# Four pairs of tiles by seven products instead of six in the last projection, with an ordered queue on each vector engine

## The chip, the cores and the metric

The kernel runs on one core of a Trainium2 chip. The metric is the time of one execution on the device, in microseconds, lower being better. The core has a matrix engine (TensorE, PE in the profile, with its weight loads as PEld), three engines that work element by element (VectorE as DVE, ScalarE as ACT, GpSimd as POOL), a queue that issues transfers (SyncE, SP) and 16 DMA engines between the off-chip memory and the core's own memory. Each engine works through its own instructions in program order and waits on semaphores that the others raise.

## The reference

The reference is one block of a sequence model on 512 tokens of width 1024: a norm, one wide projection, three token mixers, a gated merge, an output projection, and then a feed-forward part with a short convolution. All is float32. The change touches the last step only, the product by `w_down`, and what brings its operands:

```python
def conv_glu_ffn(h, w_up, w_conv, b_conv, w_down):
    a, u = jnp.split(h @ w_up, 2, axis=-1)
    return (jax.nn.gelu(dwconv3(a, w_conv, b_conv)) * u) @ w_down
...
    x = x + conv_glu_ffn(rms_norm(x, ffn_norm_g[l]), w_ffn_up[l], w_ffn_conv[l], b_ffn_conv[l], w_ffn_down[l])
return rms_norm(x, final_norm_g)
```

The hidden width is 2816, so `w_down` has 22 tiles of 128 rows and 1024 columns.

## The kernel before

**Precision.** Every float32 operand is split in a high part (a rounded copy, made by ScalarE) and a low part (the operand less the high part, made by VectorE). `mm3` (L309 to L312) makes of one product three matmuls: high by high, high by low, low by high.

**Stages.** Up to 735 us the program runs the mixers and, from L1251, a loop over 22 hidden tiles (the up stage): two projections of 24 matmuls each for a tile, then the convolution and the activation on VectorE and ScalarE, one multiply of each tile on GpSimd (L1274). From 735 us it multiplies by `w_down` (the down stage, L1354 to L1406), and after the last matmul a short tail finishes the last norm and stores.

**The down stage.** The columns are two halves of 512, the tokens two halves of 256. Of the 22 hidden tiles the first `2*NSP` are taken in pairs (p = 0 to NSP-1): a pair, the two token halves and the two column halves form a two-by-two block product, which is done with seven products in place of eight (`FORMS`, L48, numbered 1 to 7). Each of the seven forms needs a sum or a difference of token blocks (`emit_form`: a difference on VectorE, then a split in two tiles `uf`) and, except forms 2 and 5, a sum or a difference of two weight blocks. The other NOK hidden tiles are ordinary: for each column half, four token tiles by one weight tile. An item of the work is either `("s", form, pair)`, 6 matmuls of 512 columns, or `("k", column half, tile)`, 12 of them. The last three ordinary tiles of the second column half (`HELD`) are kept back and run token tile by token tile at the end. `down_items` (L54) writes the order of the items by hand: part 0 has forms 2, 4, 5, 7 and the ordinary tiles of the left half, part 1 has forms 1, 3, 6 and those of the right half; the numbers behind each form say after which pairs an ordinary tile follows.

**Weights of an item.** `weights(key)` is called as the item begins and emits, for later items: the load (`emit_raw`, on SP's queue, 256 KB for one block), the second block of a weight sum (`emit_sum`: a DMA on GpSimd's queue that adds into the tile already loaded, L236), the token block of a form (`emit_form`), and the split of the weight tile two items ahead (`emit_split`, L270 on ScalarE and L271 on VectorE). For form 1 the two weight blocks are loaded side by side and VectorE subtracts them (L247). Split weights lie in a ring of four tiles `w`; loads lie in large units (`up`, 14 units of 2112 columns for the whole kernel), four blocks in each. The first NSP items and the rest of the program use a smaller ring of three (`wr`).

**Results.** Forms 1 to 5 gather in two banks each (`at`), and `add` (L1303) adds a bank into the output blocks `C_`, four adds for a form, written behind the form's last matmul. Forms 6 and 7 and the ordinary tiles gather in four other banks (`mm`). `left` (L1320) takes the square sum of a finished left half and multiplies it by the gain, on GpSimd (L1323).

**What sets the order.** Instructions of one engine stand in an order that a scheduler chooses from the program's order and its own estimate of when operands are there; it may put a later-written instruction ahead. Only where `tc.issue_after` is used does one stand behind another by rule: before, that is so for the adding DMAs on GpSimd, behind each other and behind the multiply L1274 of the last hidden tile. The units of loads are given out in the scheduler's order too, as soon as one is free.

Of the kernel before, what the change touches and what calls it, by code (L numbers as in the profile page):

```python
# [22 lines left out]
M = 256  # L23
DFF = 2816
FT = DFF // P
NSP = 6
NOK = FT - 2 * NSP
HELD = 3
HC = D // 2
# [100 lines left out]
def hybrid_block(ctx, tc, xT, memT, wflat, vecs, gbias, nabias, out):  # L130
# [51 lines left out]

    raws, split = {}, {}
    RAW_AHEAD, SPLIT_AHEAD = 3, 1
    st = {"raw": 0, "sum": DOWN0, "form": DOWN0, "split": 0}
    uraw = []

    def emit_raw(i):
        key, n = BLOCKS[i]
        _, off, _ = BINDEX[key]  # L190
        src = wflat[off:off + P * n].rearrange("(p n) -> p n", p=P)
        if i < DOWN0 + NSP:
            r = wp.tile([P, BW], F32, tag="raw", name=nm("wr"), bufs=3)
        else:
            both = key[:2] == ("s", 1)
# [33 lines left out]

    ur, uf = [], {}  # L230

    def emit_sum(i):

        if i in st:
            with tc.issue_after(st["g"]):
                st["g"] = G.dma_start(raws[i], st.pop(i)[:, HC:], accum_op=ALU.add).ins  # L236

    def emit_form(i):

        key, n = BLOCKS[i]  # L240
        if key[0] != "s":
            return
        a, a2, _, w2, sign = FORMS[key[1]]
        p = key[2]
        if sign < 0:
            r = raws[i]
            V.tensor_tensor(r[:, :HC], r[:, :HC], r[:, HC:2 * HC], op=ALU.subtract)  # L247
        if p % 2 == 0:
            v = ur[p // 2][:, :4 * S].rearrange("p (q k s) -> p q k s", q=2, k=2)
            q2 = lambda t: t.rearrange("p (q s) -> p q s", q=2)  # L250
            src = v[:, :, a[1], a[0] * M:(a[0] + 1) * M]
            if a2:
                d = q2(scr())
                V.tensor_tensor(d, src, v[:, :, a2[1], a2[0] * M:(a2[0] + 1) * M], op=ALU.subtract)
                src = d
            h, l = [tp.tile([P, S], F32R, tag="E", name=nm("uf"), bufs=EB) for _ in range(2)]
            A.activation(q2(h), src, AF.Copy)
            V.tensor_tensor(q2(l), src, q2(h).bitcast(F32), op=ALU.subtract)
            uf[key[1], p // 2] = h, l

    def emit_split(i):
        key, n = BLOCKS[i]
        r = raws.pop(i)
        if i >= DOWN0:
            if key[0] == "k" and key[1] == 1 and key[2] >= NOK - HELD:
                h, l = lastw(key[2] - NOK + HELD)
            else:
                w = wp.tile([P, WT], F32R, tag="w", name=nm("w"), bufs=4)
                h, l = w[:, :HC], w[:, HC:2 * HC]
            A.activation(h, r[:, :HC], AF.Copy)  # L270
            V.tensor_tensor(l, r[:, :HC], h.bitcast(F32), op=ALU.subtract)  # L271
            split[i] = h, l
            return
        c, hs = halves(i)
# [972 lines left out]
    ou = [unit(F32R) for _ in range(NOK // 2)]  # L1247
    oq = lambda i: ou[i // 4][:, i % 4 * S:(i % 4 + 1) * S]
    UH, UL = [oq(2 * j) for j in range(NOK)], [oq(2 * j + 1) for j in range(NOK)]
    res, turns = {}, {}  # L1250
    for f in range(FT):  # L1251
        if f == 0:
# [18 lines left out]
        V.scalar_tensor_tensor(sq, sq, GC, c, op0=ALU.add, op1=ALU.mult)  # L1271
        A.activation(sq, sq, AF.Tanh, scale=GK)
        V.scalar_tensor_tensor(c, sq, 1.0, c, op0=ALU.add, op1=ALU.mult)  # L1273
        st["g"] = G.tensor_tensor(c, c, rb2, op=ALU.mult).ins  # L1274
        if f > 0:
            pu = pu1 if f == 1 else proj(("uu", f), HH, HL)
        if f < 2 * NSP:
            V.scalar_tensor_tensor(ur[f // 4][:, f % 4 * S:(f % 4 + 1) * S], pu, 0.5, c, op0=ALU.mult, op1=ALU.mult)
        else:
            V.tensor_tensor(c, pu, c, op=ALU.mult)  # L1280
            split_act(UH[f - 2 * NSP], UL[f - 2 * NSP], c, 0.5)
# [21 lines left out]
    def add(t, g, ps, op=ALU.add, cs=slice(0, HC)):  # L1303

        c = cv(t, g)[:, cs]
        if (t, g) in res:
            V.tensor_tensor(f4(c), res.pop((t, g)), f4(ps), op=op)
        else:
            V.tensor_tensor(c, c, ps, op=op)  # L1309

    def sums(src, v0):

# [7 lines left out]
    def left(t):  # L1320

        v1[t] = sums(cv(t, 0), EPS)
        G.tensor_tensor(cv(t, 0), cv(t, 0), gfin[0], op=ALU.mult)  # L1323

    def finish(t, ps):

# [2 lines left out]
        if t < NT - 1:  # L1329
# [21 lines left out]
            3: ((0, 1, ALU.add), (1, 1, ALU.add)), 4: ((1, 0, ALU.add), (0, 0, ALU.add)),  # L1351
            5: ((0, 0, ALU.add), (0, 1, ALU.subtract))}
    last = NT - 1
    for n, key in enumerate(DOWN):  # L1354
        wh, wl = weights(key)
        if key[0] == "s":
            _, i, p = key
            if p == 0 and i < 6:
# [6 lines left out]
            if i < 6 and p == NSP - 1:  # L1365
                for th, g, op in adds[i]:
                    for u in range(2):
                        add(2 * th + u, g, pm[u], op)
                if i == 1:
                    for t in range(2):  # L1370
                        left(t)
            continue
        _, g, j = key
        if j == 0:
# [2 lines left out]
        if not held:  # L1377
# [3 lines left out]
                    j == NOK - 1 if g == 0 else t == last and j == NOK - HELD - 1)  # L1381
            if g == 0 and j == NOK - 1:
                for t in range(NT):
                    add(t, 0, px[t])
                for t in range(2, NT):
                    left(t)
            continue
        res["w", j] = wh, wl
        if j < NOK - 1:
            continue  # L1390
        add(last, 1, px[last])
        for t in range(NT):
            tsl = slice(t * P, (t + 1) * P)
# [118 lines left out]
```

## Time and profile before

| | |
|---|---|
| median of 3 runs | 872.5 us (870.56 to 872.68) |
| profiled execution | 871.15 us |
| its span, first to last instruction | 869.4 us |
| before and behind the span | 1.75 us |
| TensorE busy, share of the span | 851.0 us, 98% |
| VectorE, ScalarE, GpSimd busy | 619.4, 464.1, 160.1 us |
| down stage, first to last matmul | 735.08 to 860.4 us |

The page's busy time of PE counts a matmul from its start to a modelled end, so 98% does not say that TensorE runs at its pace; the stretches in which it works at half clock count as busy too. Three views carry the reading: a table of stretches with the busy time of each engine, the instructions in order of time, and the waits of one engine for another. In a row of the table of stretches the numbers are the length, then for PE, PEld, DVE, ACT and POOL the busy time and in brackets the count of instructions, then the granted TensorE clock, the busy share of the 16 DMA engines and GB/s. In a row of the instructions in order of time they are the start, the duration, engine, line, operation, tiles (out<-in), and in square brackets the idle time ahead of it with what ended it.

### The profile page before, as it was taken

How to read it: one execution, taken by the hardware profiler on the slowest of the kernel's cores; microseconds unless marked ns; L12 is line 12 of the kernel's file. 1: busy time of each engine (PE TensorE's matmuls, PEld its weight loads, DVE VectorE, ACT ScalarE, POOL GpSimd, SP SyncE). 2: the span in 40 equal slices, each digit the busy share in tenths (PEclk: the TensorE clock that was granted, in tenths of full speed). 3: DMA queues.
4: the chain of work that ended last, by engine and by line, in shares of the span. 5: the costliest groups of instructions: out<-in, count | busy, mean ns of one | idle time of the engine just before them, and what ended most of it. 6: DMA issues, size and time to landing. Idle time of an engine off the chain costs nothing.

```text
span 869.4 us, 12253 instructions
## 1 busy us (share of the span) xinstructions
PE 851.0 (98%) x4044; PEld 713.2 (82%) x4044; DVE 619.4 (71%) x1235; ACT 464.1 (53%) x975; POOL 160.1 (18%) x243
## 2 busy tenths in 40 slices
PE   9999999999999999999999999999999999899885
PEld 7898888988888888888888888888888888787764
DVE  7699677874467668997585567766666668877663
ACT  7465556775355658887544444444444445444342
POOL 2001100000104810742001202111111111221401
PEclk9999999999999999999999999999999999999999
DMA  8237644643435846887523423544432225975932
GB/s 271 96 101 226 210 160 144 206 135 98 133 122 171 226 137 212 228 241 213 194 97 124 142 85 100 162 145 139 143 98 96 97 92 174 245 203 154 253 74 98
DMA packets 76978, 135.76 MB, mean 156 GB/s; under 512 B 10217, under 2 KB 35433, under 8 KB 76913
## 3 DMA queue, kind: packets, MB, share of 16 engines
q1 hardware_dynamic: 65808, 122.22, 43.4%
q0 software_dynamic: 10816, 12.61, 7.7%
q8 instruction: 32, 0.52, 0.3%
q14 instruction: 34, 0.27, 0.1%
q10 hardware_dynamic: 288, 0.14, 0.1%
HBM read 120.23 MB, written 14.70 MB: 155 GB/s over the span
## 4 chain that ended last, share of the span: by engine, by line
PE 89%; DMA 3%; issue 3%; DVE 3%; ACT 1%; POOL 1%; SPq 0%; POOLq 0%; DVEq 0%; ACTq 0%
PE mm L311 25%; PE mm L310 25%; PE mm L312 25%; DMA u<-wflat 3%; PE at L311 3%; PE at L312 2%; PE at L310 2%; DVE w L271 1%; PE at L958 1%; PE at L791 1%; PE at L793 1%; PE at L775 1%; POOL s L1274 0%; PE at L925 0%; PE at L924 0%
## 5 line engine op out<-in xcount | busy, mean ns | idle before, releaser
L310 PE MATMUL mm<-u,w 128*128 128x512 f32 (+1 forms) x912 | 353.8, 388 | 0.0
L312 PE MATMUL mm<-u,w 128*128 128x512 f32 (+1 forms) x912 | 352.0, 386 | 0.0
L311 PE MATMUL mm<-u,w 128*128 128x512 f32 (+1 forms) x912 | 351.9, 386 | 0.0
L285 ACT ACTIVATE w<-wr 128x512 fp32r<-128x512 f32 (+1 forms) x256 | 159.9, 628 | 145.7 <-PE mm L312 110.8
L286 DVE TENSOR_TENSOR w<-wr,w 128x512 fp32r<-128x512 f32 (+2 forms) x257 | 176.1, 689 | 69.8 <-ACT w L285 66.8
L312 PEld LDWEIGHTS mm<-u,w 128*128 128x128 f32 x912 | 171.3, 188 | 35.4 <-DVE w L286 0.7
L310 PEld LDWEIGHTS mm<-u,w 128*128 128x128 f32 x912 | 171.5, 188 | 33.7 <-ACT u L316 0.3
L311 PEld LDWEIGHTS mm<-u,w 128*128 128x128 f32 x912 | 171.4, 188 | 33.3 <-DVE u L317 0.5
L604 POOL DMA_DIRECT2D u<-nav_d x128 | 62.3, 506 | 101.0 <-PE at L958 51.9
L1274 POOL TENSOR_TENSOR s<-s,rb 128x512 f32<-128x512 f32 x22 | 37.9, 1721 | 190.0 <-DVE s L1273 182.3
L271 DVE TENSOR_TENSOR w<-u,w 128x512 fp32r<-128x512 f32 x53 | 40.5, 779 | 23.5 <-ACT w L270 23.3
L270 ACT ACTIVATE w<-u 128x512 fp32r<-128x512 f32 x53 | 32.9, 626 | 41.3 <-PE mm L312 26.6
L311 PE MATMUL mm<-w,u 128*128 128x512 f32 x116 | 46.1, 397 | 3.5 <-DVE w L271 3.5
L310 PE MATMUL mm<-w,u 128*128 128x512 f32 x116 | 46.2, 398 | 0.0
L312 PE MATMUL mm<-w,u 128*128 128x512 f32 x116 | 45.9, 396 | 0.0
L236 POOL DMA_DIRECT2D u<-wflat x24 | 21.4, 1175 | 62.4 <-DVE u L1309 27.3
L311 PEld LDWEIGHTS mm<-w,u 128*128 128x128 f32 x116 | 22.2, 192 | 8.9 <-DVE w L271 4.3
L497 ACT ACTIVATE s<-pad,vec 128x512 f32<-128x512 f32 x30 | 24.4, 813 | 5.4 <-DVE pad L495 4.4
L311 PE MATMUL at<-w,uf 128*128 128x512 f32 x60 | 24.3, 404 | 2.9 <-DVE w L271 2.9
L312 PEld LDWEIGHTS mm<-w,u 128*128 128x128 f32 x116 | 22.2, 191 | 4.7
L1242 POOL TENSOR_TENSOR acc<-acc,s 128x512 f32<-128x512 f32 x7 | 9.0, 1290 | 92.4 <-ACT s L1241 92.4
L310 PEld LDWEIGHTS mm<-w,u 128*128 128x128 f32 x116 | 22.2, 192 | 4.6
(301 smaller groups left out, 1197.3 us busy)
## 6 DMA issues: line engine op xcount, KB each, us to landing
wr<-wflat SPq DMA_DIRECT2D x124, 512.0 KB, 3.4
u<-wflat SPq DMA_DIRECT2D x50, 256.0 KB, 5.4
td<-s SPq DMA_DIRECT2D x160, 64.0 KB, 2.0
U<-td SPq DMA_DIRECT2D x40, 256.0 KB, 3.6
s<-xT SPq DMA_DIRECT2D x24, 256.0 KB, 4.4
u<-wflat POOLq DMA_DIRECT2D x24, 256.0 KB, 8.4
nab<-nabias SPq DMA_DIRECT2D x16, 256.0 KB, 3.9
u<-nav_d POOLq DMA_DIRECT2D x128, 32.0 KB, 3.6
```

The source lines that it names most:

```text
L236: st["g"] = G.dma_start(raws[i], st.pop(i)[:, HC:], accum_op=ALU.add).ins
L270: A.activation(h, r[:, :HC], AF.Copy)
L271: V.tensor_tensor(l, r[:, :HC], h.bitcast(F32), op=ALU.subtract)
L285: A.activation(h[:, u:v], src, AF.Copy)
L286: V.tensor_tensor(l[:, u:v], src, h[:, u:v].bitcast(F32), op=ALU.subtract)
L310: PE.matmul(ps, lh, rh, start=start, stop=False)
L311: PE.matmul(ps, lh, rl, start=False, stop=False)
L312: st["mm"] = PE.matmul(ps, ll, rh, start=False, stop=stop).ins
L497: A.activation(t1, pad[:, 0:512], AF.Identity, scale=vcol(w, i), bias=vcol(b, i))
L604: G.dma_start(vw[r * 32:(r + 1) * 32, i * 256:(i + 1) * 256], nav_v[hf, r, CW[b]:CW[b] + 32, hp * 256:(hp + 1) * 256])
L1242: G.tensor_tensor(acc2, acc2, sq, op=ALU.add)
L1274: st["g"] = G.tensor_tensor(c, c, rb2, op=ALU.mult).ins
```

## The change

It does five things.

- `NSP` is 4 in place of 6: eight hidden tiles are taken in pairs by seven products, and 14 in place of 10 are ordinary. The lists of `down_items` put one ordinary tile behind almost every pair of a form.
- `in_turn` issues an instruction of VectorE, ScalarE or GpSimd behind the last one that it issued on the same engine. The differences and splits of token blocks, the splits of weights, the adds and the adding DMAs go through it, so that they stand on each engine in the order in which they are written.
- `emit_form` is cut in two: `emit_diff` (differences of token blocks and of form 1's weights, up to 3 and then 4 items ahead) and `emit_form` (their splits, 3 ahead); weights are split between the two. The adding DMAs are asked for 7 items ahead in place of 5.
- The adds of a finished form or column half go on a list, `todo`; at each item one of them is emitted, or two while more than two are waiting. The multiply of `left` moves from GpSimd to VectorE.
- In the up stage the units of ordinary hidden tiles are taken one at a time; hidden tiles 8 to 11 are now split there (L317 and L316 of the kernel before) where they were stored whole (L1278).

```diff
-NSP = 6
+NSP = 4
...
-                if p in at:
+                for _ in range(at.count(p)):
...
-    part(0, ((2, (4, 5)), (4, (1, 3, 5)), (5, (2, 5)), (7, (1, 3, 5))))
-    part(1, ((1, (2, 4, 5)), (3, (2, 5)), (6, (2, 5))))
+    part(0, ((2, (3, 3)), (4, (0, 1, 2, 3)), (5, (0, 1, 2, 3)), (7, (0, 1, 2, 3))))
+    part(1, ((1, (1, 1, 2, 3)), (3, (0, 1, 2, 3)), (6, (0, 1, 3))))
...
+OWN_SUM = (1,)
...
+    chain = {}
+
+    def in_turn(eng, what, *a, **k):
+
+        with tc.issue_after(chain[eng]) if eng in chain else ExitStack():
+            chain[eng] = getattr({"V": V, "A": A, "G": G}[eng], what)(*a, **k).ins
+
     def emit_sum(i):

         if i in st:
-            with tc.issue_after(st["g"]):
-                st["g"] = G.dma_start(raws[i], st.pop(i)[:, HC:], accum_op=ALU.add).ins
+            in_turn("G", "dma_start", raws[i], st.pop(i)[:, HC:], accum_op=ALU.add)
...
-            V.tensor_tensor(r[:, :HC], r[:, :HC], r[:, HC:2 * HC], op=ALU.subtract)
+            in_turn("V", "tensor_tensor", r[:, :HC], r[:, :HC], r[:, HC:2 * HC], op=ALU.add if sign > 0 else ALU.subtract)
...
+    def emit_form(i):
+
+        key, n = BLOCKS[i]
+        if key[0] == "s" and key[2] % 2 == 0:
+            f = key[1], key[2] // 2
             h, l = [tp.tile([P, S], F32R, tag="E", name=nm("uf"), bufs=EB) for _ in range(2)]
-            A.activation(q2(h), src, AF.Copy)
-            V.tensor_tensor(q2(l), src, q2(h).bitcast(F32), op=ALU.subtract)
-            uf[key[1], p // 2] = h, l
+            in_turn("A", "activation", q2(h), uf[f], AF.Copy)
+            in_turn("V", "tensor_tensor", q2(l), uf[f], q2(h).bitcast(F32), op=ALU.subtract)
+            uf[f] = h, l
...
-            A.activation(h, r[:, :HC], AF.Copy)
-            V.tensor_tensor(l, r[:, :HC], h.bitcast(F32), op=ALU.subtract)
+            in_turn("A", "activation", h, r[:, :HC], AF.Copy)
+            in_turn("V", "tensor_tensor", l, r[:, :HC], h.bitcast(F32), op=ALU.subtract)
...
-        while st["sum"] <= min(i + 5, st["raw"] - 1):
+        while st["sum"] <= min(i + 7, st["raw"] - 1):
             emit_sum(st["sum"])
             st["sum"] += 1
+        while st["diff"] <= min(i + 3, last):
+            emit_diff(st["diff"])
+            st["diff"] += 1
+        while st["split"] <= min(i + (2 if st["split"] >= DOWN0 else SPLIT_AHEAD), last):
+            emit_split(st["split"])
+            st["split"] += 1
         while st["form"] <= min(i + 3, last):
             emit_form(st["form"])
             st["form"] += 1
-        while st["split"] <= min(i + (2 if st["split"] >= DOWN0 else SPLIT_AHEAD), last):
-            emit_split(st["split"])
-            st["split"] += 1
+        while st["diff"] <= min(i + 4, last):
+            emit_diff(st["diff"])
+            st["diff"] += 1
...
-        G.tensor_tensor(cv(t, 0), cv(t, 0), gfin[0], op=ALU.mult)
+        in_turn("V", "tensor_tensor", cv(t, 0), cv(t, 0), gfin[0], op=ALU.mult)
...
+    todo = []
+
+    def work(n):
+
+        for _ in range(min(n, len(todo))):
+            todo.pop(0)()
+
     for n, key in enumerate(DOWN):
         wh, wl = weights(key)
+        work(2 if len(todo) > 2 else 1)
...
-                        add(2 * th + u, g, pm[u], op)
+                        todo.append(lambda t=2 * th + u, g=g, ps=pm[u], op=op: add(t, g, ps, op))
```

The diff does not show where the scheduler now puts the instructions; three places of the built programs do. In their rows stand the line, the operation and the tiles, out<-in, with the number of each tile; L238 is the line of `in_turn`, so a row there is told by its tiles.

The first place is VectorE near the start of the down stage, from the low part of the weights of form 4's first pair to that of its second pair. Before, `w_7349` and `w_7364` are these two; `s_` are differences of token blocks and `u_7246` is an output block that takes adds:

```order
L271 TENSOR_TENSOR w_7349<-u_7283,w_7349 128x512
L254 TENSOR_TENSOR s_7466<-u_5381 128x512
L254 TENSOR_TENSOR s_7496<-u_5382 128x512
L254 TENSOR_TENSOR s_7541<-u_5383 128x512
L254 TENSOR_TENSOR s_7586<-u_5381 128x512
L1307 TENSOR_TENSOR u_7246<-U_6173,at_7256 128x512
L1307 TENSOR_TENSOR u_7246<-U_6260,at_7257 128x512
L1307 TENSOR_TENSOR u_7246<-U_6509,at_7256 128x512
L1307 TENSOR_TENSOR u_7246<-U_6591,at_7257 128x512
L271 TENSOR_TENSOR w_7364<-u_7283,w_7364 128x512
```

After, the same two are `w_7320` and `w_7360`; `w_7343` is the ordinary tile between them and `u_7255` the output block:

```order
L238 TENSOR_TENSOR uf_7310<-u_5381,uf_7309 128x512
L238 TENSOR_TENSOR w_7320<-u_7262,w_7320 128x512
L238 TENSOR_TENSOR u_7255<-U_6170,at_7274 128x512
L238 TENSOR_TENSOR u_7255<-U_6259,at_7275 128x512
L238 TENSOR_TENSOR w_7343<-u_7262,w_7343 128x512
L238 TENSOR_TENSOR u_7255<-U_6514,at_7274 128x512
L238 TENSOR_TENSOR w_7360<-u_7267,w_7360 128x512
L238 TENSOR_TENSOR u_7255<-U_6596,at_7275 128x512
L238 TENSOR_TENSOR w_7374<-u_7267,w_7374 128x512
```

The four differences are gone from this place, and the four adds stand in twos and ones between the splits of weights.

The second place is ScalarE in the last form. Before, `w_7974`, `w_7985` and `w_8002` are the high parts of weights that are used next, `u_8136` those of the three tiles that are held to the end:

```order
L270 ACTIVATE w_7959<-u_7831 128x512
L270 ACTIVATE u_8136<-u_8028 128x512
L270 ACTIVATE w_7974<-u_7831 128x512
L270 ACTIVATE u_8136<-u_8028 128x512
L257 ACTIVATE uf_8015<-s_8013 128x512
L270 ACTIVATE w_7985<-u_7831 128x512
L270 ACTIVATE u_8136<-u_8028 128x512
L270 ACTIVATE w_8002<-u_7831 128x512
```

After, the held tiles are `u_8082`:

```order
L238 ACTIVATE w_8049<-u_7877 128x512
L238 ACTIVATE w_8058<-u_7952 128x512
L238 ACTIVATE w_8073<-u_7952 128x512
L238 ACTIVATE u_8082<-u_7952 128x512 x2
L238 ACTIVATE u_8082<-u_8015 128x512
L1339 ACTIVATE s_8121,y_8122<-u_7254 128x512
```

The held tiles moved behind the last weights that are used before them.

The third place is GpSimd in the same stretch. Before, the multiplies of `left` stand between the adding DMAs:

```order
L236 DMA u_7751<-wflat 128x512
L1323 TENSOR_TENSOR u_7246<-u_7246,gf_7247 128x512
L236 DMA u_7751<-wflat 128x512 x2
L1323 TENSOR_TENSOR u_7246<-u_7246,gf_7247 128x512
L236 DMA u_7831<-wflat 128x512 x3
```

After, only DMAs are left there:

```order
L238 DMA u_7683<-wflat 128x512
L238 DMA u_7731<-wflat 128x512 x2
L238 DMA u_7816<-wflat 128x512 x2
L238 DMA u_7877<-wflat 128x512 x2
L238 DMA u_7952<-wflat 128x512
```

The multiplies went to VectorE, and the sums in a unit are two at most, where they were three.

More of the change, by code (lines that the diff above doesn't have):

```diff
@@ L184, in hybrid_block @@
     RAW_AHEAD, SPLIT_AHEAD = 3, 1
-    st = {"raw": 0, "sum": DOWN0, "form": DOWN0, "split": 0}
+    st = {"raw": 0, "sum": DOWN0, "form": DOWN0, "diff": DOWN0, "split": 0}
     uraw = []
@@ L194, in emit_raw @@
         else:
-            both = key[:2] == ("s", 1)
+            both = key[0] == "s" and key[1] in OWN_SUM
             if both and len(uraw) % 2:
@@ L1246, in hybrid_block @@
     ur.extend(unit() for _ in range(NSP // 2))
-    ou = [unit(F32R) for _ in range(NOK // 2)]
-    oq = lambda i: ou[i // 4][:, i % 4 * S:(i % 4 + 1) * S]
-    UH, UL = [oq(2 * j) for j in range(NOK)], [oq(2 * j + 1) for j in range(NOK)]
+    ou, UH, UL = [], [], []
     res, turns = {}, {}
@@ L1273, in hybrid_block @@
         V.scalar_tensor_tensor(c, sq, 1.0, c, op0=ALU.add, op1=ALU.mult)
[L1274 removed]
+        chain["G"] = G.tensor_tensor(c, c, rb2, op=ALU.mult).ins
         if f > 0:
@@ L1280, in hybrid_block @@
             V.tensor_tensor(c, pu, c, op=ALU.mult)
-            split_act(UH[f - 2 * NSP], UL[f - 2 * NSP], c, 0.5)
+            if f % 2 == 0:
+                ou.append(unit(F32R))
+            for i, part in enumerate((UH, UL)):
+                a = f % 2 * 2 + i
+                part.append(ou[-1][:, a * S:(a + 1) * S])
+            split_act(UH[-1], UL[-1], c, 0.5)
         if 3 <= f < 11:
@@ L1367, in hybrid_block @@
                     for u in range(2):
-                        add(2 * th + u, g, pm[u], op)
+                        todo.append(lambda t=2 * th + u, g=g, ps=pm[u], op=op: add(t, g, ps, op))
                 if i == 1:
-                    for t in range(2):
-                        left(t)
+                    todo.extend(lambda t=t: left(t) for t in range(2))
             continue
@@ L1383, in hybrid_block @@
                 for t in range(NT):
-                    add(t, 0, px[t])
-                for t in range(2, NT):
-                    left(t)
+                    todo.append(lambda t=t, ps=px[t]: add(t, 0, ps))
+                todo.extend(lambda t=t: left(t) for t in range(2, NT))
             continue
@@ L1390, in hybrid_block @@
             continue
+        work(len(todo))
         add(last, 1, px[last])
```

16 lines of the change are left out of this document (9 added, 7 removed).

## The prediction

> **What bounds the kernel now.** I read the table of stretches first, for the stretch in which TensorE stops working at its pace. Up to the down stage there is none: at 600 us, where the edits to the up stage lie, PE fills its time. From 735 us I cut the stretches at the places where matmul starts lie apart.
>
> ```profile
> 600.00:620.00 20.00, 20.00 (x90) 16.57 (x89) 14.04 (x21) 8.15 (x13) 3.25 (x2) 1.00 0.48 147
> ...
> 735.08:749.80 14.72, 14.72 (x66) 12.20 (x65) 10.73 (x19) 7.90 (x14) 7.62 (x7) 1.00 1.07 320
> 749.80:757.00 7.20, 4.82 (x14) 3.50 (x13) 7.20 (x13) 2.41 (x4) 0.86 (x1) 0.76 0.82 162
> 757.00:803.30 46.30, 46.30 (x206) 38.30 (x204) 34.54 (x53) 21.32 (x37) 7.10 (x9) 1.00 0.66 183
> 803.30:812.00 8.70, 5.98 (x20) 4.43 (x18) 7.41 (x9) 2.34 (x5) 2.62 (x4) 0.80 0.82 184
> 812.00:826.75 14.75, 14.75 (x66) 12.20 (x65) 7.60 (x14) 5.40 (x11) 9.47 (x11) 1.00 1.08 287
> 826.75:836.20 9.45, 6.20 (x22) 3.63 (x21) 6.65 (x11) 7.14 (x13) 0.74 (x1) 1.00 0.70 146
> 836.20:860.40 24.20, 24.20 (x116) 20.31 (x114) 12.62 (x22) 5.99 (x12) 1.12 (x2) 1.00 0.06 23
> 735.08:860.40 125.32, 116.96 (x502) 94.58 (x500) 86.74 (x137) 52.49 (x95) 29.52 (x31) 0.97 0.67 176
> 860.40:869.40 9.00, 0.15 (x2) 0.00 (x0) 3.44 (x11) 2.72 (x8) 1.08 (x2) 0.80 0.47 177
> ```
>
> The weight loads (second bracket) count the matmuls of a stretch. At 757 us, undisturbed, 204 take 46.30 us: **0.227 us each**. By that pace three stretches hold lost time:
>
> - at 750 us: 7.20 - 13 x 0.227 = 4.25 us
> - at 803 us: 8.70 - 18 x 0.227 = 4.61 us
> - at 827 us: 9.45 - 21 x 0.227 = 4.68 us
>
> Together **13.54 us** of the 125.32; elsewhere the stage is bound by TensorE. The next view, instructions in order of time, says why each happens.
>
> *At 750 us* the order of VectorE is at fault.
>
> ```profile
> 746.00 0.63 ACT L270 ACTIVATE w<-u 128x512 fp32r<-128x512 f32 x1 [4.08 <-PE at L311]
> ...
> 747.27 2.49 DVE L254 TENSOR_TENSOR s<-u 128x512 f32<-128x512 f32 x4
> 749.68 2.48 DVE L1307 TENSOR_TENSOR u<-U,at 128x512 f32<-128x512 f32 x4
> 752.07 1.29 DVE L271 TENSOR_TENSOR w<-u,w 128x512 fp32r<-128x512 f32 x2
> ...
> 752.81 0.54 PE L311 MATMUL at<-w,uf 128*128 128x512 f32 x1 [2.38 <-DVE w L271]
> ```
>
> Four differences and four adds, 4.9 us, stand ahead of the low part for which PE waits. The wait is 2.38 us; the rest of the 4.25 is the clock, 0.76 in this stretch.
>
> *At 803 us* one VectorE instruction takes 5.53 us where the same operation else takes 0.69.
>
> ```profile
> 800.81 5.53 DVE L271 TENSOR_TENSOR w<-u,w 128x512 fp32r<-128x512 f32 x1
> ...
> 801.13 1.62 POOL L1323 TENSOR_TENSOR u<-u,gf 128x512 f32<-128x512 f32 x1
> ...
> 802.38 2.12 POOL L236 DMA_DIRECT2D u<-wflat  x2
> ...
> 803.52 2.26 POOL L1323 TENSOR_TENSOR u<-u,gf 128x512 f32<-128x512 f32 x1
> ...
> 806.40 0.50 PE L311 MATMUL mm<-w,u 128*128 128x512 f32 x1 [2.72 <-DVE w L271]
> ```
>
> It ends at 806.34, 0.6 us after the second multiply of `left` on GpSimd; I read it as kept out by these two. PE waits 2.72 us and then again runs at a lower clock (0.80).
>
> *At 827 us* ScalarE stands for 6.59 us at the load of a held tile, with nearer weights queued behind, and transfers are late: the DMA engines are full from 812 us (share 1.08).
>
> ```profile
> 827.65 0.63 ACT L270 ACTIVATE u<-u 128x512 fp32r<-128x512 f32 x1 [6.59 <-DMA u<-wflat]
> ...
> 828.85 0.51 PE L310 MATMUL at<-w,uf 128*128 128x512 f32 x1 [1.71 <-ACT w L270]
> ```
>
> Here the waits are several short ones, the longest 1.71 us, and the clock stays at 1.00.
>
> So waits of 2.38 and 2.72 us are followed by slow matmuls, and one of 1.71 us is not. [...]
>
> **The change part by part.**
>
> *Matmuls.* Two pairs less are 2 x 7 x 6 = 84 matmuls less; four ordinary tiles more are 4 x 2 x 12 = 96 more. 12 x 0.227 = **+2.72 us**, all on the path.
>
> *Order of VectorE.* Behind the first summed weights there now stand two adds, not eight instructions. A form's adds are spread over the next items, and no PE work waits for them soon: a form's banks are used again two forms on. Gone: -4.25. New waits by the order: an add waits for its form's last matmul with the next weight splits behind it; those are needed two items later, 4 to 7 us, and the adds take 0.6 us each, so 0.
>
> *`left` on VectorE.* Four multiplies of 0.69 us in place of GpSimd's; nothing but DMA issues stays on GpSimd up to the tail. Do issues alone hold VectorE up? Near the start six of them ran beside it:
>
> ```profile
> 736.65 2.28 POOL L1274 TENSOR_TENSOR s<-s,rb 128x512 f32<-128x512 f32 x1 [9.61 <-DVE s L1273]
> 738.87 5.39 POOL L236 DMA_DIRECT2D u<-wflat  x6
> ...
> 739.57 1.28 DVE L271 TENSOR_TENSOR w<-wr,w 128x512 fp32r<-128x512 f32 x2
> 740.77 0.68 DVE L317 SCALAR_TENSOR_TENSOR u<-s,u 128x512 fp32r<-128x512 f32 x1
> ```
>
> They did not. Gone: -4.61.
>
> *Transfers.* The queues over 735 to 855 us (120 us):
>
> ```profile
> q1 hardware_dynamic: 7504, 15.22, 36.8%
> q0 software_dynamic: 3456, 6.29, 31.3%
> ...
> u<-wflat SPq DMA_DIRECT2D x41, 256.0 KB, 5.6
> u<-wflat POOLq DMA_DIRECT2D x24, 256.0 KB, 8.4
> ```
>
> A plain block of 0.262 MB costs 36.8% x 120 / (15.22 / 0.262) = 0.76 us of all engines, an adding one 31.3% x 120 / 24 = 1.57. A form with sums was 6 x 2.33 + 3 x 0.76 = 16.3 us of transfers beside 6 x 6 + 3 x 12 = 72 matmuls, 16.3 us: no reserve. It becomes 4 x 2.33 + 4 x 0.76 = 12.4 us beside 4 x 6 + 4 x 12 = 72, 16.3 us: 76%. So no backlog builds up, and the held tiles are split last. Gone: -4.68. Priced from below, were the transfers alone not enough, this term would be 0; that is a rival.
>
> *Splits and the up stage.* Six weight splits, seven token splits, five differences and two differences of form 1 go, 20 VectorE instructions of 0.69 us against four multiplies more: nothing, as PE covers it (VectorE is busy 86.74 of 125.32 us). In the up stage four tiles need one VectorE and one ScalarE instruction more, 0.7 us in a step of 11 us with 6 us of VectorE idle in 20: nothing; without that cover it would be 4 x 0.7 = 2.8.
>
> *What is late next.* The first adding DMA goes out at 738.87, behind GpSimd's last multiply, and its tile was split at 746.00 at the latest landing. That tile was the ninth item, due at 735.08 + 72 - 12 = 60 matmuls x 0.227 = 748.7. Now it is the seventh, due after 48 matmuls, at **745.96**. With the same landing its high part ends at 746.63 and its low part at 747.35, 1.2 us behind the second matmul; the bounds: nothing with the shortest landing of the view of this line, 4.1 us, and with the median at the start, 9.8, a wait of 738.87 + 9.8 + 1.4 - 745.96 = 4.1, with 1.9 us of slow clock (4.25 - 2.38) 6.0.
>
> ```profile
> DMA to landing us min/median/max: 4.1/8.4/13.2
> ...
> u<-wflat POOLq DMA_DIRECT2D x7, 256.0 KB, 9.8
> ```
>
> I take **+1.2**, since 746.00 is a row of this very transfer.
>
> *Tail.* 9.00 us, as before: the same instructions stand there.
>
> **Sum.** 871.15 (the profiled execution, 869.4 span + 1.75) - 13.54 + 2.72 + 1.2 = **861.5 us**. The profiled execution lies 1.35 below the median of the runs, within their spread; I leave the forecast at 861.5.
>
> **The rivals.**
>
> *A: the first sum is later than that,* behind the loads of four units that go out in one go, as now: 866.3 (6.0 in place of 1.2). Against it: the first units hold the four sums of form 4, and form 5 has none, where six went out before.
>
> *B: GpSimd's DMA issues, not its multiplies, held the 5.53 us.* Two issues do lie inside it. Then one such stop comes back: 861.5 + 4.6 = 866.1. Against it: the six issues above. [...]
>
> *C: the strict order makes a wait of its own,* or the third gap stays because it was one of landing alone: one gap in place of none, 861.5 + 4.7 = 866.2.
>
> *D, the slower side: three units for loads.* Of 14 units, seven ordinary, two paired and two output units leave three; before, five, three and two left four. A unit is loaded again once its fourth tile is split; eight tiles lie ahead, of which two are split already: 6 items x 9 matmuls x 0.227 = 12.3 us. By the stage's medians load and sum take 5.6 + 8.4 = 14.0, 1.7 late, over nine reloads 15.6: 877.1. It turns slower by 0.3% from 13.7 us. Against it: in the quieter stretch, 757 to 800 us, with the load on the DMA engines (0.66) that I expect, they take 3.7 + 5.7 = 9.4:
>
> ```profile
> u<-wflat SPq DMA_DIRECT2D x14, 256.0 KB, 3.7
> ...
> u<-wflat POOLq DMA_DIRECT2D x5, 256.0 KB, 5.7
> ```
>
> *E: the slow matmuls have a cause other than the waits ahead of them and stay:* 4.25 + 4.61 - 2.38 - 2.72 = 3.8 us, 865.3. Against it: outside the three stretches the clock is 1.00.
>
> **How the numbers follow.** Forecast 0.62, A 0.12, B 0.08, C 0.10, D 0.05, E 0.03. The range: with no new wait 860.3, less 1.5 for the spread of the runs: 858.8; the dearest single rival on the faster side 866.2 to 866.3 and 1.35 from profiled to median: 867.5. A measurement here tells 0.3%, 2.6 us, from no change. Slower is D, 0.05; for no change I take 0.03 out of A, B, C and E, two or more at once; faster 0.92.
>
> **What would show it.** In the changed profile the down stage should start at 735 us, hold 12 matmuls more and end near 850, with PE's starts 0.227 us apart throughout and the clock at 1.00 from 750 us on. VectorE should have no instruction of over 1 us there (B), GpSimd no multiply; the adding DMAs' median landing should fall below 8.4 us (D, third gap). A wait of PE for low parts at 746 to 748 us of up to 2 us is the new term; more is A. I am wrong if PE waits again at form ends (C) or at the first tile of a unit (D).

## The result and the profile after

| | before | after |
|---|---|---|
| median | 872.36 us (870.56 to 872.68, 4 runs) | 863.39 us (863.19 to 863.60, 4 runs) |
| profiled execution, its span | 871.15, 869.4 us | 863.51, 861.4 us |
| down stage, first to last matmul | 735.08 to 860.40: 125.32 us | 736.50 to 851.96: 115.46 us |
| from there to the end of the span | 9.00 us | 9.44 us |

The ratio after to before is 0.9901, with a 95% interval of 0.9884 to 0.9919: about 1% faster, 9 us. The forecast was 861.5 us, its range 858.8 to 867.5.

The table of stretches of the changed kernel, in the columns of before:

```profile
600.00:620.00 20.00, 20.00 (x90) 16.53 (x90) 14.88 (x24) 8.67 (x14) 3.25 (x2) 1.00 0.42 127
736.50:747.43 10.93, 10.93 (x49) 8.82 (x47) 4.50 (x8) 4.03 (x8) 5.27 (x5) 1.00 1.00 291
747.43:750.52 3.09, 2.72 (x10) 1.72 (x10) 3.09 (x6) 2.67 (x5) 0.00 (x0) 1.00 0.87 158
750.52:851.96 101.44, 101.44 (x457) 84.31 (x455) 64.85 (x108) 38.60 (x69) 11.51 (x14) 1.00 0.51 140
736.50:851.96 115.46, 115.09 (x514) 94.85 (x512) 72.43 (x120) 45.29 (x81) 16.77 (x19) 1.00 0.56 155
851.96:861.40 9.44, 0.16 (x2) 0.00 (x0) 3.46 (x11) 2.74 (x8) 1.08 (x2) 0.66 0.45 168
```

The three stretches with lost time are gone, and the granted clock is 1.00 through the stage. The DMA engines, though, are as full late in the stage as before. The first row is before, the second after (the share adds up the time of all packets, so it can pass 1):

```profile
812.00:822.00 10.00, 10.00 (x46) 8.26 (x45) 7.02 (x14) 5.40 (x11) 5.94 (x7) 1.00 1.06 299
```

```profile
812.00:822.00 10.00, 10.00 (x46) 8.29 (x45) 7.50 (x14) 4.20 (x9) 3.39 (x4) 1.00 1.09 301
```

One short stretch with lost time is new, at 747 us. The instructions in order of time show it:

```profile
746.75 1.15 ACT L238 ACTIVATE w<-u 128x512 fp32r<-128x512 f32 x2 [4.82 <-DMA u<-wflat]
747.41 0.69 DVE L238 TENSOR_TENSOR w<-u,w 128x512 fp32r<-128x512 f32 x1 [4.59 <-ACT w L238]
...
748.02 1.28 DVE L238 TENSOR_TENSOR u<-U,at 128x512 f32<-128x512 f32 x2
...
748.16 0.50 PE L333 MATMUL at<-w,uf 128*128 128x512 f32 x1 [0.23 <-DVE w L238]
...
749.22 0.68 DVE L238 TENSOR_TENSOR w<-u,w 128x512 fp32r<-128x512 f32 x1
```

The first summed tile lands at 746.7, ScalarE and VectorE split it one after the other, and the second matmul of form 4 waits for the low part. The low part of the next ordinary tile then stands behind two adds, and its matmul starts late too, at 749.96. From matmul start to matmul start the two places lose 1.07 us, about 0.6 and 0.4. The stage is 9.86 us shorter, where the forecast's terms (-13.54 + 2.72 + 1.2) give 9.62.

The rest of the difference lies outside the stage. It began 1.42 us later than in the profiled execution of before, and this was there before the up stage. The same matmul of both kernels, before and after:

```profile
427.24 0.40 PE L310 MATMUL mm<-u,w 128*128 128x512 f32 x1
```

```profile
428.66 0.40 PE L332 MATMUL mm<-u,w 128*128 128x512 f32 x1
```

The edits do not touch this part of the program. Of the 1.42 us, 0.55 are there by 20 us, while the first loads come in, and two places at 302 and 384 us add 0.25 and 0.55. The 14 kernels of this study, with one profiled execution each, start the stage between 735.08 and 737.24; that of experiment 1, whose one edit lies near 800 us, starts it at 735.79, so 0.7 us can come without any edit ahead of the stage. Whether all of the 1.42 us is such variation was not tested. With 0.44 us more behind the last matmul and 0.36 us more around the span, -9.86 + 1.42 + 0.44 + 0.36 = -7.64, which is 863.51 less 871.15.

### The profile page after: what moved, and what is told of

It is laid out like the page before. It is cut to its first block, busy times and chain, and to the rows that moved or that the text cites. A ratio compares the mean times of both kernels' runs of the same rounds, so it can differ in the third digit from the quotient of the medians.

```text
span 861.4 us, 12205 instructions
## 1 busy us (share of the span) xinstructions
PE 849.9 (99%) x4056; PEld 713.5 (83%) x4056; DVE 608.0 (71%) x1223; ACT 459.1 (53%) x966; POOL 147.7 (17%) x231
## 4 chain that ended last, share of the span: by engine, by line
PE 94%; issue 2%; DMA 1%; DVE 1%; ACT 1%; POOL 0%; SPq 0%; POOLq 0%; ACTq 0%
PE mm L334 27%; PE mm L333 27%; PE mm L332 27%; PE at L332 3%; PE at L333 3%; PE at L334 3%; PE at L980 1%; DMA u<-wflat 1%; PE at L813 1%; DMA wr<-wflat 1%; PE at L815 1%; PE at L797 1%; PE at L947 0%; PE at L946 0%; PE at L757 0%
## 5 line engine op out<-in xcount | busy, mean ns | idle before, releaser
L238 ACT ACTIVATE w<-u 128x512 fp32r<-128x512 f32 x49 | 30.7, 631 | 57.4 <-PE mm L334 40.8
L333 PE MATMUL mm<-w,u 128*128 128x512 f32 x148 | 57.7, 390 | 0.1
L332 PE MATMUL mm<-w,u 128*128 128x512 f32 x148 | 57.8, 390 | 0.0
L334 PE MATMUL mm<-w,u 128*128 128x512 f32 x148 | 57.6, 389 | 0.0
L238 DVE TENSOR_TENSOR w<-u,w 128x512 fp32r<-128x512 f32 x49 | 33.7, 689 | 32.5 <-ACT w L238 32.1
L333 PEld LDWEIGHTS mm<-w,u 128*128 128x128 f32 x148 | 27.8, 188 | 6.2 <-DVE w L238 0.6
L334 PEld LDWEIGHTS mm<-w,u 128*128 128x128 f32 x148 | 27.8, 188 | 5.8
L332 PEld LDWEIGHTS mm<-w,u 128*128 128x128 f32 x148 | 27.8, 188 | 5.7
L338 ACT ACTIVATE u<-s 128x512 fp32r<-128x512 f32 x14 | 8.9, 633 | 36.1 <-DVE s L1300 36.1
L238 POOL DMA_DIRECT2D u<-wflat x16 | 14.0, 994 | 66.9 <-DVE s L238 22.6
L520 DVE SCALAR_TENSOR_TENSOR s<-pad,vec,s 128x512 f32<-128x512 f32 x30 | 22.5, 749 | 4.0 <-ACT s L519 4.0
```

The source lines that it names most:

```text
L238: chain[eng] = getattr({"V": V, "A": A, "G": G}[eng], what)(*a, **k).ins
L332: PE.matmul(ps, lh, rh, start=start, stop=False)
L333: PE.matmul(ps, lh, rl, start=False, stop=False)
L334: st["mm"] = PE.matmul(ps, ll, rh, start=False, stop=stop).ins
L338: A.activation(h, src, AF.Copy, scale=scale)
L520: V.scalar_tensor_tensor(t1, pad[:, 1:513], vcol(w, n + i), t1, op0=ALU.mult, op1=ALU.add)
```

## The experiments

Each was timed beside runs of the kernel before, whose median was 871.9 to 872.2 us in them. "Six pairs in turn" is the changed kernel with `NSP = 6` and the lists of before (experiment 3); several others start from it.

**1. `left` on VectorE, alone.**

```diff
 before, in left():
-        G.tensor_tensor(cv(t, 0), cv(t, 0), gfin[0], op=ALU.mult)
+        V.tensor_tensor(cv(t, 0), cv(t, 0), gfin[0], op=ALU.mult)
```

> The kernel before with one edit: the four multiplies of left are on VectorE. Theory (GpSimd's two multiplies kept VectorE's split out for 5.53 us): the stop at 803 us is gone, VectorE's longest instruction there is 0.7 us, time 872.4 - 4.6 = 867.8 us; the stretches at 750 and 827 us stay as they were. Rival (the two adding-DMA issues on GpSimd kept it out): an instruction of some 5 us is still there, time 872.4 us. Second rival (the stop only hid lateness of transfers that the next stretch then shows): the stop goes, but the stretch at 827 us grows by as much, 872.4 us.

Measured: 871.8 us against 872.0, ratio 1.000 (0.9982 to 1.0018). The waits of TensorE in the down stage, in total, times and longest:

```profile
PE at L310 <- ACT w L270: 4.3, 1, 4.3
PE at L311 <- DVE w L271: 2.5, 1, 2.5
PE mm L311 <- DVE w L271: 1.0, 1, 1.0
```

The wait at 803 us is gone, and no VectorE instruction in the stage takes over 0.78 us, though the adding DMAs are still issued by GpSimd. So the multiplies were what kept VectorE out for the 5.53 us of before. But nothing was won that the interval shows: ScalarE, ahead of the held tile, now waits longer.

```profile
815.06 0.63 ACT L270 ACTIVATE w<-u 128x512 fp32r<-128x512 f32 x1 [0.56 <-ACT s L1314]
824.91 0.63 ACT L270 ACTIVATE u<-u 128x512 fp32r<-128x512 f32 x1 [9.22 <-DMA u<-wflat]
825.44 0.61 ACT L270 ACTIVATE w<-u 128x512 fp32r<-128x512 f32 x1
```

Before it waited 6.59 us, up to 827.65. In this execution TensorE had lost 6.1 us less by then (1.5 us of it because no slow matmuls followed the wait at 753 us: from the second on they start 0.22 to 0.24 us apart, where it was 0.43 before, which the edit does not explain), but counted from the start of the stage the held tile's load came only 3.4 us earlier. Much of what TensorE gained it waits off here: one wait of 4.3 us, with eight matmuls 0.43 us apart behind it, and the third stretch grows from 4.7 us to 8.6. The second rival's numbers came out.

**2. Four pairs and their lists, alone.** `NSP`, the two `part` lines, the count in `down_items` and the single units, put into the kernel before; nothing is ordered.

> The kernel before with four pairs and the new lists, and the units of ordinary tiles taken singly; VectorE and ScalarE keep the scheduler's order, the adds are written at the form's end and left stays on GpSimd. Theory (three separate causes): only the stretch at 827 us goes with the smaller load of transfers: 872.4 - 4.7 + 2.7 (12 matmuls) + 1.1 (first sum late) = 871.5 us, with waits of over 2 us behind four adds or beside GpSimd's multiplies still in the trace. Rival (the tiles and lists do it all): 863 to 864 us, no such wait.

Measured: 867.72 us, ratio 0.9955 (0.9937 to 0.9973), between the two. The theory was wrong about which stretch would go: the long wait left is the third.

```profile
PE mm L310 <- ACT w L270: 3.2, 1, 3.2
PE mm L311 <- DVE w L271: 0.3, 1, 0.3
PE at L311 <- DVE w L271: 0.2, 1, 0.2
```

It stands at 822 to 825 us, behind ScalarE's wait of 6.37 us for the held tile's load. So fewer adding DMAs, 16 in place of 24, do not remove the third stretch; they do not empty the DMA engines ahead of it either:

```profile
812.00:822.00 10.00, 10.00 (x45) 8.07 (x43) 4.22 (x9) 3.33 (x9) 4.75 (x6) 1.00 1.09 294
```

The first two stretches, on the other hand, are all but gone (0.8 us is left, at 746 us) without any ordered queue. Beside GpSimd's multiplies two VectorE instructions still take 1.7 and 1.8 us, and TensorE does not wait for them.

**3. Six pairs in turn.**

```diff
 after:
-NSP = 4
+NSP = 6
-    part(0, ((2, (3, 3)), (4, (0, 1, 2, 3)), (5, (0, 1, 2, 3)), (7, (0, 1, 2, 3))))
-    part(1, ((1, (1, 1, 2, 3)), (3, (0, 1, 2, 3)), (6, (0, 1, 3))))
+    part(0, ((2, (4, 5)), (4, (1, 3, 5)), (5, (2, 5)), (7, (1, 3, 5))))
+    part(1, ((1, (2, 4, 5)), (3, (2, 5)), (6, (2, 5))))
```

> The changed kernel with six pairs and the lists of before; the ordered queues, the single adds and left on VectorE stay. Theory (transfers are the cause of the third stretch): the first two stretches are gone, the third stays with 4 to 5 us, DMA share near 1 from 800 to 827 us: 863.4 - 2.7 (12 matmuls less) - 1.1 (first sum two items later) + 4.7 = 864.3 us. Rival (order alone did it, here too by putting the held tiles last): 859.6 us, TensorE at its pace through all the stage.

Measured: 858.22 us (858.06 to 858.62), ratio 0.9845 (0.9829 to 0.9860). This is faster than the changed kernel by 5.2 us, and the rival's forecast rather than the theory's. Its table of stretches:

```profile
735.72:795.00 59.28, 59.28 (x263) 49.10 (x262) 46.50 (x74) 29.08 (x48) 12.29 (x13) 1.00 0.78 219
795.00:810.00 15.00, 15.00 (x68) 12.43 (x67) 12.91 (x24) 8.37 (x16) 5.21 (x6) 1.00 0.98 250
810.00:825.00 15.00, 15.00 (x68) 12.42 (x67) 13.30 (x25) 7.96 (x15) 5.18 (x6) 1.00 1.10 279
825.00:847.36 22.36, 22.36 (x108) 18.81 (x106) 12.30 (x21) 8.16 (x16) 1.12 (x2) 1.00 0.16 43
735.72:847.36 111.64, 111.64 (x502) 92.76 (x500) 85.01 (x140) 53.59 (x95) 23.81 (x27) 1.00 0.73 196
```

TensorE keeps its pace from first to last: 111.64 us, which is 125.32 less the 13.54 us of lost time, to within 0.14. The DMA engines are as full as before (1.10 from 810 to 825 us; the 14.75 us before the third stretch of the kernel before had 1.08). Plain loads issued from 802 to 818 us even land later, by the median 12.8 us against 6.1 before (the first row is before, the second this kernel):

```profile
u<-wflat SPq DMA_DIRECT2D x16, 256.0 KB, 6.1
```

```profile
u<-wflat SPq DMA_DIRECT2D x12, 256.0 KB, 12.8
```

TensorE waits for none of them. ScalarE now takes the tiles in the order in which they are needed, and it splits the three held tiles at 833.07 us, without a wait:

```profile
833.07 1.66 ACT L238 ACTIVATE u<-u 128x512 fp32r<-128x512 f32 x3
```

**4. `left` back on GpSimd, four pairs,** and **7. the same with six pairs.**

```diff
 after, in left():
-        in_turn("V", "tensor_tensor", cv(t, 0), cv(t, 0), gfin[0], op=ALU.mult)
+        in_turn("G", "tensor_tensor", cv(t, 0), cv(t, 0), gfin[0], op=ALU.mult)
```

> The changed kernel with left's multiplies back on GpSimd, in its queue between the adding DMAs. Theory (multiplies keep VectorE out): one or two VectorE instructions of 2 to 5.5 us while they run and TensorE waits behind one: 863.4 + up to 4.6 = 868.0 us; where the multiplies come in pairs, the stop is the longer. Rival (issues, not multiplies, or nothing of the kind): 863.4 us, no VectorE instruction over 1 us.

> Six pairs in turn (858.2 us) with left's multiplies back on GpSimd, one adding DMA between two of them. Theory (a VectorE split stands still as long as GpSimd's multiply runs, and through a run of multiplies with issues between): a split of 2 to 5.5 us near 800 us and again near 815 us, TensorE waits where it exceeds the two items of reserve: 858.2 to 862.8 us. Rival (only 1 to 1.7 us as with four pairs, hidden by the reserve): 858.2 us.

Measured: 862.1 us (0.9892; 0.9876 to 0.9907) with four pairs, no slower than the changed kernel, and 858.8 us (0.9845; 0.9829 to 0.9861) with six. TensorE loses nothing near the multiplies in the one and 0.27 us in the other. The rivals held. In the first, VectorE and GpSimd at two of the multiplies:

```profile
802.17 1.73 POOL L238 TENSOR_TENSOR u<-u,gf 128x512 f32<-128x512 f32 x1 [2.59 <-ACT s L1339]
...
802.75 1.70 DVE L238 TENSOR_TENSOR w<-u,w 128x512 fp32r<-128x512 f32 x1
...
813.38 1.62 POOL L238 TENSOR_TENSOR u<-u,gf 128x512 f32<-128x512 f32 x1
813.44 1.28 DVE L238 TENSOR_TENSOR u<-u,at 128x512 f32<-128x512 f32 x2
```

The split beside the first of these took 1.70 us, 1.0 over its usual 0.69; the two adds beside the second, which read `at`, took their usual 0.64 us each. The 5.53 us of before came from two multiplies with two DMA issues between them, all in a row. With six pairs two multiplies stand as close, with one issue between them, and hold two VectorE instructions for 1.72 and 2.21 us, of which the reserve of two items covers all but the 0.27 us. Why one split stood through both multiplies before is not shown.

**5. The eight VectorE instructions put back, six pairs in turn.**

```diff
 six pairs in turn:
+        work(len(todo) if n == 7 else 2 if len(todo) > 2 else 1)
         wh, wl = weights(key)
-        work(2 if len(todo) > 2 else 1)
...
-        while st["diff"] <= min(i + 3, last):
+        while st["diff"] <= min(i + (18 if i == DOWN0 + 7 else 3), last):
```

> Six pairs in turn (858.2 us), with the four adds of form 2 and four differences written between the low parts of form 4's first two weight tiles, as they stood before. Theory (these eight alone made the stretch at 750 us): TensorE waits some 2.4 us for the second low part and then runs slow for about 2 us: 858.2 + 4.2 = 862.4 us. Rival (the wait came from the load of transfers or of six adding DMAs at the start, which is there either way): 858.2 us, no wait over 0.5 us.

Measured: 859.8 us (0.9857; 0.9842 to 0.9873), 1.6 us more than six pairs in turn; the stage loses 2.0 us at one place.

```profile
747.59 2.47 DVE L238 TENSOR_TENSOR u<-U,at 128x512 f32<-128x512 f32 x4
749.98 2.49 DVE L238 TENSOR_TENSOR s<-u 128x512 f32<-128x512 f32 x4
752.39 1.28 DVE L238 TENSOR_TENSOR w<-u,w 128x512 fp32r<-128x512 f32 x2
```

These are the eight again, and TensorE waits 1.72 us behind them. The cause of the first stretch is shown, its size not: no slow matmuls follow, from the second on they start 0.22 to 0.24 us apart.

**12. All adds of a form at once, six pairs in turn.** `work(len(todo))` in place of one or two.

> Six pairs in turn (858.2 us), but a form's four adds (and what follows them on the list) are written at once at the next item in place of singly. Theory (adds matter only where they stand with differences ahead of a split that is due: eight instructions cost a wait of 1.7 us, so four, 2.4 us of VectorE shorter, cost none): 858.2 us, no wait over 0.5 us. Rival (VectorE has so little reserve with six pairs that every bunch shows): 1 to 2 us at each of the six forms' ends, 860 to 865 us.

Measured: 860.24 us (0.9856; 0.9825 to 0.9887), 2.0 us more. TensorE loses 0.93 and 0.70 us at two places, 752 and 829 us, each time behind a bunch of adds (2.48 us for four) ahead of a split, and 0.1 us each at 801 and 815 us. The theory missed; the rival's time came out at its lower end, with two places in place of six and less at each.

**6. ScalarE freed, six pairs in turn.**

```diff
 six pairs in turn, in in_turn():
-        with tc.issue_after(chain[eng]) if eng in chain else ExitStack():
+        with tc.issue_after(chain[eng]) if eng != "A" and eng in chain else ExitStack():
```

> Six pairs in turn (858.2 us), but ScalarE's instructions are no longer tied to one another, so the scheduler puts the held tiles' splits ahead of nearer weights again; VectorE and GpSimd stay in turn. Theory (ScalarE's order is the cause of the stretch at 827 us): ScalarE stands some 6 us at a load between 815 and 825 us, TensorE waits 2 to 4 us and runs slow: 858.2 + 4.7 to 6.5 = 863 to 865 us. Rival (transfers were the cause and VectorE's order has relieved them): 858.2 us.

Measured: 871.5 us (0.9993; 0.9980 to 1.0006): all that six pairs in turn had won is lost, 13.3 us.

```profile
825.82 0.63 ACT L238 ACTIVATE u<-u 128x512 fp32r<-128x512 f32 x1 [13.67 <-DMA u<-wflat]
826.35 0.61 ACT L238 ACTIVATE w<-u 128x512 fp32r<-128x512 f32 x1
827.00 0.69 DVE L238 TENSOR_TENSOR w<-u,w 128x512 fp32r<-128x512 f32 x1 [13.15 <-ACT w L238]
827.02 0.29 PEld L332 LDWEIGHTS mm<-w,u 128*128 128x128 f32 x1 [10.53 <-ACT w L238]
827.02 0.80 PE L332 MATMUL mm<-w,u 128*128 128x512 f32 x1 [10.11 <-ACT w L238]
```

One split of a held tile stands in front of the next weights, and its load lands at 825.8 us. TensorE, with only 0.4 us lost earlier (8.9 in the kernel before), arrives early and waits 10.11 us, then runs at half clock (0.50) for 6.5 us. The theory had the cause and half the size.

**9. ScalarE in turn, alone.**

```diff
 before:
+    def act(out, src):
+
+        with tc.issue_after(st["a"]) if "a" in st else ExitStack():
+            st["a"] = A.activation(out, src, AF.Copy).ins
...
-            A.activation(q2(h), src, AF.Copy)
+            act(q2(h), src)
...
-            A.activation(h, r[:, :HC], AF.Copy)
+            act(h, r[:, :HC])
```

> The kernel before with one edit: ScalarE's splits of weights and token blocks stand in the order in which they are written, so the held tiles come last. Transfers, six pairs, GpSimd's multiplies and VectorE's rules are those of before. Theory (ScalarE's order exposes the late loads, and any earlier stop only shifts what it shows): the stretch at 827 us is gone and the two others stay: 872.0 - 4.7 = 867.3 us. Rival (transfers are late whatever the order): 872 us, TensorE waiting for other weights near 827 us.

Measured: 862.69 us, ratio 0.9898 (0.9881 to 0.9914), a gain of 9.5 us, as much as the whole change. No wait of TensorE is long:

```profile
PE at L316 <- DVE w L276: 1.6, 3, 0.8
PE at L315 <- ACT w L235: 0.6, 1, 0.6
```

The third stretch is gone, with the DMA engines as full as before (1.09 from 812 to 822 us). Some 4.1 us are left in short pieces, the larger ones 1.3 at 741 us, 0.9 at 753, 0.4 at 783 and 1.4 at 806 us. So the first two stretches shrank too, from 8.9 us to 2.3. At 753 the scheduler, with ScalarE tied, put two differences less in front of the low part, and TensorE came there later, by what it had lost at 741. At 801 a split and a difference beside GpSimd's multiplies took 1.7 and 2.2 us; no split took 5.5:

```profile
800.87 1.71 DVE L276 TENSOR_TENSOR w<-u,w 128x512 fp32r<-128x512 f32 x1
802.51 2.24 DVE L259 TENSOR_TENSOR s<-u 128x512 f32<-128x512 f32 x1
```

At neither place do slow matmuls follow: from the third on they start 0.22 to 0.24 us apart. Why the multiplies hold VectorE less here was not separated from the shifted times. So of the 9.5 us only the third stretch, 4.7, is shown to be ScalarE's order itself.

**8. Form 5 second.**

```diff
 after:
-    part(0, ((2, (3, 3)), (4, (0, 1, 2, 3)), (5, (0, 1, 2, 3)), (7, (0, 1, 2, 3))))
+    part(0, ((2, (3, 3)), (5, (0, 1, 2, 3)), (4, (0, 1, 2, 3)), (7, (0, 1, 2, 3))))
```

> The changed kernel (863.4 us) with form 5, which needs no sums, run ahead of form 4, so that the first summed tile is due 16 us later. Theory (the first sum's landing costs 1.1 us at 747 to 750 us): that wait is gone, TensorE at its pace from 736 us to the end of the stage: 862.3 us. Rival (the wait is the queue of four loads and four adding DMAs at the start and comes whatever is first): 863.4 us.

Measured: 862.12 us (0.9885; 0.9868 to 0.9903), 1.3 us under the changed kernel, though the two intervals overlap. The trace is clearer: its stage takes 114.36 us, 1.10 less, with no gap between matmul starts:

```profile
737.24:751.60 14.36, 14.36 (x65) 11.91 (x64) 11.77 (x19) 6.92 (x12) 4.36 (x4) 1.00 0.93 265
751.60:851.60 100.00, 100.00 (x451) 83.13 (x449) 60.70 (x101) 38.60 (x70) 12.41 (x15) 1.00 0.53 142
```

So the wait at 747 us is the first sum's.

**10 and 11. Eight pairs in turn,** with `NSP = 8` and lists to match; in 11 also `OWN_SUM = (1, 3)`.

> Eight pairs, all in turn, sums by adding DMAs; 12 matmuls less than six pairs. If transfers have reserve: 858.2 - 2.7 = 855.5 us. By the price of one adding block (1.57 + 0.76 us of all engines) a form with sums has 8 x 2.33 + 1.5 x 0.76 = 19.8 us of transfers beside 66 matmuls, 15.0 us, and the whole stage 108 us beside 109: waits for late sums of some us in forms 4, 7 and 6, 858 to 865 us.

> Eight pairs, all in turn; form 3's weight blocks are loaded side by side and added by VectorE as form 1's are, the rest by adding DMAs. Part 1 has 13.3 us of transfers in two forms and 19.8 in one: if the transfers were the limit there, it is gone and the time is 855.5 us plus what form 4 and 7 still wait, 855.5 to 861 us. Rival (VectorE is now the limit: 15.8 us of its work in form 3 beside 15.0 us of matmuls): waits on VectorE in form 3, slower than eight pairs without it.

Measured: 864.01 us (0.9910; 0.9894 to 0.9926) and 867.64 us (0.9946; 0.9928 to 0.9964). Here the reserve ends, though not where it was expected. With eight pairs TensorE waits 2.8 us at 745 us for the weights of form 2's last pair, a plain load that goes through the ring of three, and a little behind it runs slow (eight matmuls 0.40 to 0.43 us apart); later, from 806 us, it loses 3.0 us in pieces of 0.2 to 0.6 us, and the waits that the view names there are for VectorE's low parts, none for transfers. With form 3's sums on VectorE such places get more, above all from 808 to 832 us, as the rival had it. What the late load at 745 us alone costs was not tried. Six pairs is the best that was run.

## Why the prediction held, and where its reasons did not

The time lay inside the range, 1.9 us over the forecast. The stage came out 0.24 us better than its terms, and the start and the tail, which the sum took as unchanged, 2.2 us worse in the profiled execution. But the prediction gave part of the gain to the wrong edits, and that its sum came out close is partly luck.

- *Matmuls, +2.72.* Right. The changed kernel's stage less that of six pairs in turn is 115.46 - 111.64 = 3.82 us: 2.72 for the twelve matmuls, 1.07 for the first sum.
- *What is late next, +1.2.* Right as to the cause: gone when form 5 goes first (8). That 1.07 us is so near is luck. The sum was in ScalarE's hands 10.25 us after the start of the stage, where 10.92 was assumed, so the place named lost 0.6 us only; the other 0.4 is the next ordinary tile behind two adds, which the forecast did not have.
- *Order of VectorE, -4.25.* Right as to the cause (5), too large as a share. The eight instructions alone cost a wait of 1.72 us, 1.6 us of time. The slow matmuls, the rest of the 4.25, follow some waits and not others (2.38 us before, but neither 1.72 in 5 nor 2.52 in 1). The order is also not the only way: four pairs and their lists took this stretch down to 0.8 us without it (2). That the order makes no new waits was right but for the 0.4 us above, and the single adds are worth 2.0 us with six pairs (12).
- *`left` on VectorE, -4.61.* That the multiplies made the instruction of 5.53 us was right (0.78 at most without them, 1), the sum was not: alone it won 0.2 us (1), less than its interval, and with everything else in turn taking it back cost nothing with four pairs and 0.6 us with six (4, 7). Against rival B: with the multiplies gone, 16 issues of adding DMAs in the changed kernel left no VectorE instruction over 0.78 us.
- *Transfers, -4.68.* **This step failed.** It said "A form with sums was 6 x 2.33 + 3 x 0.76 = 16.3 us of transfers beside 6 x 6 + 3 x 12 = 72 matmuls, 16.3 us: no reserve", and of four pairs "So no backlog builds up, and the held tiles are split last." Only the last half of that counts. The 76% of four pairs is an average over a form; in the changed kernel the share was 0.51 from 757 to 800 us, but 1.09 from 812 to 822, where the kernel before had 1.06, and the plain loads issued from 802 to 818 us landed after 9.2 us by the median, not 6.1. So a backlog did build up, and it cost nothing. It costs nothing with six pairs in turn either (share 1.10, 3), and with four pairs and ScalarE's order free the stretch stays (2). ScalarE's order decides: with it alone the third stretch is gone (9), and without it alone 13.3 us are lost (6). The prediction named that wait of 6.59 us, and then priced the load on the DMA engines.
- *The sum of the three.* -13.54 was right only because all three went. They are not independent. The last waits for a load that reached ScalarE at 827.7, 824.9 and 825.8 us where TensorE had lost 8.9, 2.8 and 0.4 us before (the kernel before, 1, 6): it moves far less than TensorE does, so what is won earlier is mostly waited off there.
- *Rivals.* A, D and E did not happen, and of C only the 0.4 us. For D, the stage has no gap after 750.5 us, so the three units were reloaded in time. The fall of the adding DMAs' median landing, 8.4 to 6.8 us, came as forecast, but it was not what bound.

So beside the ordered queues two pairs less is the part of the change that costs: 3.8 us in the stage, 5.2 between the medians, of which some 1.4 us lie before the stage and behind it. Without them the same four pairs and lists win 4.3 us (2). The ordered queues are the part that pays, ScalarE's above all. Asking for the adding DMAs 7 items ahead in place of 5, and cutting `emit_form` in two, were never run apart from the rest.

## What to carry to other kernels

Where an engine splits or copies operands in order of arrival, look at what stands behind its longest wait for a transfer: an operand that is needed late, in front of one that is needed soon, turns a harmless backlog of transfers into a stop (here 13.3 us, experiment 6). Look at the load on the DMA engines where the wait is, not at its average. Lost stretches in a row must not be added up as if each edit kept its own: if the last one waits for a load that lands hardly earlier, gains made before it are waited off there (here its load reached ScalarE at 824.9 to 827.7 us, whether TensorE had lost 0.4 or 8.9 us by then), so undo it first, or test the edits in pairs. When a change bundles an order with a new amount of work, run the order with the old amount; here that was the fastest version, 858.22 us.

## What the runs showed of the hardware that was not expected

- *Half clock behind a wait of TensorE (matmuls 0.43 us apart in place of 0.227) is not decided by the length of the wait alone.* Waits of 1.71 and 1.72 us had no slow matmuls behind them, those of 2.38, 2.72, 2.8, 3.2, 4.3 and 10.1 us had, but one of 2.52 us (experiment 1, at 753.66) had none. In the kernel before the 2.72 us were followed by about five matmuls at pace and then seven at 0.43 us. From 7 to 12 matmuls in a row at 0.43 us, 3.0 to 5.1 us, were seen. What decides it besides the length no run here shows.
- *Beside a GpSimd multiply a VectorE split, with both operands in the core's memory, took 1.70 us and not 0.69, while two adds that read the matmul's banks took their usual 0.64 us each* (experiment 4). That the place of the operands makes the difference is the author's reading of these rows; no run varied it alone. The 5.53 us of before lasted through two multiplies and the two issues between, and no run here shows why.
- *When a late stage begins differs between profiles by as much as some of the terms argued about:* the down stage began between 735.08 and 737.24 us in the 14 kernels, and 0.7 us apart in two that are alike up to 800 us (before and experiment 1).
